# Four small edits around the FFN of a two-layer streaming encoder: stores begun from ScalarE, one more tile buffer, a split priority, two planned waits

## The chip, the cores and the metric

The kernel runs on one core of a Trainium2 chip. The metric is the device time of one execution in microseconds; a kernel's time is the median over its runs. All arithmetic is 32-bit: a product of two 32-bit operands is made of three TensorE matmuls on float32r parts (high x high, high x low, low x high), so every weight and every activation that goes into a matmul is first split into a rounded high part (a cast on ScalarE) and the remainder (a subtraction on VectorE).

## The reference

One step of a hybrid encoder on 1024 prompt rows and 64 sample rows (1088 columns here, since the kernel keeps everything transposed), width 1024, FFN width 2816. Layer 0 is a Mamba-2 SSD mixer and a SwiGLU FFN, layer 1 is chunk-band attention and a SwiGLU FFN; every sub-layer has a norm before and after.

```python
def rmsnorm(x, w):
    y = x * lax.rsqrt(jnp.mean(x * x, axis=-1, keepdims=True) + EPS)
    return y * w
def swiglu(u, w_in, w_out):
    g, up = jnp.split(u @ w_in, 2, axis=-1)
    return (jax.nn.silu(g) * up) @ w_out
for layer in range(2):
    nw = norm_w[layer]
    m = ssd_mixer(rmsnorm(x, nw[0]), ...) if layer == 0 else attention(rmsnorm(x, nw[0]), ...) @ w_o
    x = x + rmsnorm(m, nw[1])
    x = x + rmsnorm(swiglu(rmsnorm(x, nw[2]), ffn_w_in[layer], ffn_w_out[layer]), nw[3])
```

## The kernel before

**Order.** TensorE's program order is written out by hand: the Python code emits its instructions one after the other, and a planner (`Stream`, `st`) keeps a planned time `st.t` that grows with every matmul. Side tasks (generators) yield a delay in planned microseconds and go on when `st.t` has passed it; what such a task then emits for TensorE stands at that place in its order. The other queues (VectorE, ScalarE, GpSimd and the DMA issues of SyncE) are ordered by a scheduler at build time, by readiness and by emission order; `tc.high_priority(n)` lets an instruction count as emitted `n` places earlier. Every queue is then executed in order. `paced` ties an instruction to TensorE's present place, for the scheduler only.

**Columns.** The 1088 columns stand in four slices `QS` of 256, 256, 288 and 288 (q = 0 to 3), two blocks `b` of 512 and 576 (b = 0 holds q = 0 and 1), and, for the projections, three slices `SL`.

**First FFN stage** (`back`). The 22 tiles of the hidden width are worked in three groups. `T_PLAIN`, six tiles (0, 1, 2 and 11, 12, 13), is multiplied in the ordinary way for the first block only (`plain_pairs`, L1385 gate, L1389 product). `T_BOTH`, 16 tiles, goes through `run_pair` for both blocks; `T_TAIL`, which is the same six tiles as `T_PLAIN`, goes through `run_pair` for the second block. `run_pair` makes one gate tile and one up tile of both halves of a block by seven half-size products in the manner of Strassen, in the order P1, P6, P2, P7, P5, P4, P3. VectorE takes each product out of PSUM: P7 into `u3` (L1436), P5 into `c22` and `u2` (L1439, L1440), P4 (L1442 to L1444), P3 (L1446, L1447). The px pool has four PSUM tiles. The tiles `u3` of the first block share their two buffers with the second column half `x` of the plain tiles (tag `u30`).

**Hidden tiles** go to a scratch in HBM, `hscr` (`hidden`, `out`, `store`, L1475): for a tile of the first half (number below 11) two stores, the value and a difference; for a tile of the second half five stores, two values and three sums that GpSimd makes (L1481). A store is spawned with a planned delay of 4.0. The second stage reads the scratch back (L1512) and splits it (L1518, L1519).

**Weights** (`Weights`): loads into two raw tiles (L283, SyncE), sums of them for the seven products (L332, L333, L350, L351), and splits (`part`, L386 cast on ScalarE, L387 subtraction on VectorE) under `tc.high_priority(self.pri)`. `pri` is `HIP` = 3000 at the turn to paired tiles, 0 in most of the first stage and `LDP` in the second FFN stage.

**Second FFN stage.** Seven products over 11 tiles each, for both blocks (`po`, L1756 to L1758), the last of them, P4, first for block 0 and then for block 1, with weights held in the tiles `r`. As a slice's result is complete, `end` normalises it (L1584), adds the residual (L1585) under `tc.high_priority(ENP[q])`, `ENP` = (1000, 2500, 1500, 800), and stores it. In layer 0 `end` goes on to split the result for the projections (L1540, L1541), sums its squares (L1610 to L1616, `ssum`), and, after a planned wait `EQ_W[q]`, emits the second root: TensorE transposes the sums (L564, `nst`), VectorE makes the inverse root (L575 to L588, `nv`, `nr`), TensorE spreads it (L594, `nbp`) and ScalarE copies it (L597). The keys, values and queries of slice s are scaled by it (`evk`, L1898).

Of the kernel before, what the change touches and what calls it, by code (L numbers as in the profile page):

```python
# [8 lines left out]
F32 = mybir.dt.float32  # L9
# [7 lines left out]
P = 128  # L17
# [30 lines left out]
ST_W, ST_RB = (6.5, 22.0, 22.0), (6.0, 1.0, 1.0)  # L48
TB_W, TB_V = 1.0, 10.0
OS = 1.9, 1.4  # L50
EP_W, ER_W, EQ_W = (6.0, 5.0, 8.0, 6.0), (6.0, 4.0, 6.0, 5.0), (8.0, 9.0, 18.0, 16.0)

HIP = 3000
BYP = 0, 0, 800, 800
CHP, OPP = ((300, 1500), (1500, 1500)), ((0, 1200), (1200, 1200))
LDP, ENP, ATP = 1500, (1000, 2500, 1500, 800), 1000
RWP = 3000, 0, 0

KBUF, NPRE = 5, 3
# [10 lines left out]
T_PLAIN = tuple(t for k in range(NB0 // 2) for t in (k, k + KH))  # L70
T_BOTH = tuple(t for k in range(NB0 // 2, KH) for t in (k, k + KH))
T_TAIL = tuple(range(NB0 // 2)) + tuple(range(KH, KH + NB0 // 2))
HO = 0, 256
# [349 lines left out]
def hybrid_kernel(  # L423
# [4 lines left out]
    nc = tc.nc  # L428
    V, A, G, PE = nc.vector, nc.scalar, nc.gpsimd, nc.tensor
# [3 lines left out]
    def pool(es, name, bufs=1, **kw):  # L433
        return es.enter_context(tc.tile_pool(reuse_waits="tile", name=name, bufs=bufs, **kw))
# [49 lines left out]
    def paced(x):  # L484
        if at_pe[0] is not None:
            tc.add_manual_dep(x.ins, at_pe[0].ins.name, NS, reason="pace")
        return x
# [28 lines left out]
    def mm(name):  # L516
        return pmm.tile([P, 512], F32, tag="mm", name=name)
# [212 lines left out]
    with ExitStack() as es:  # L730
# [413 lines left out]
        for s in range(NSL):  # L1144
            us, n = u[s], SL[s][1]
# [251 lines left out]
    def run_pair(t_, pr, bs, ends, ops, hid, px, tmp, apart=False, keep=None):  # L1397


        tb = {b: {} for b in bs}  # L1400
        for (p_, key, c0, i), b in [(x, b) for b in bs for x in PRODS] if apart else [(x, b) for x in PRODS for b in bs]:
            h, v = pr[key]
            n, x = ops[b].n, tb[b]

            def t_new(tag):
                if tag == "u3" and keep is not None:
                    return keep[:, t_ * n:(t_ + 1) * n]
                return tmp.tile([P, n], F32, tag=f"{tag}{b}", bufs=2 if tag == "u3" or (tag == "p1" and not b) else 1, name=tag)

            st.wait_for(lambda: i in ops[b].hl)  # L1410
            ah, al = ops[b].hl[i]
            ps = (px.tile([P, 512], F32, tag="mm", name="px") if p_ != P1 else mm("px"))[:, :n]
            for k in range(4):
                wh, wl = h[:, c0 + k * P:c0 + (k + 1) * P], v[:, c0 + k * P:c0 + (k + 1) * P]
                PE.matmul(ps, wh, ah[:, k, :], start=(k == 0), stop=False)  # L1415
                PE.matmul(ps, wh, al[:, k, :], start=False, stop=False)  # L1416
                at_pe[0] = PE.matmul(ps, wl, ah[:, k, :], start=False, stop=(k == 3))  # L1417
                if k == 1:
                    st.run(6 * n / MMR)
            st.t += 6 * n / MMR  # L1420
            if b in ends:
                for r in ops[b].rings[i]:
                    r.put()
            with tc.high_priority(HIP):
                if p_ == P1:
                    x["p1"] = t_new("p1")
                    A.copy(x["p1"], ps)
                elif p_ == P6:
                    x["u2"] = t_new("u2")
                    V.tensor_tensor(x["u2"], ps, x["p1"], op=ALU.add)  # L1430
                elif p_ == P2:
                    V.tensor_tensor(x["p1"], ps, x["p1"], op=ALU.add)
                    A.activation(x["p1"], x["p1"], AF.Silu)
                elif p_ == P7:
                    x["u3"] = t_new("u3")
                    V.tensor_tensor(x["u3"], ps, x["u2"], op=ALU.add)  # L1436
                elif p_ == P5:
                    x["c22"] = t_new("c22")
                    V.tensor_tensor(x["c22"], ps, x["u3"], op=ALU.add)  # L1439
                    V.tensor_tensor(x["u2"], ps, x["u2"], op=ALU.add)  # L1440
                elif p_ == P4:
                    V.tensor_tensor(ps, ps, x["u3"], op=ALU.add)  # L1442
                    A.activation(ps, ps, AF.Silu)
                    V.tensor_tensor(x["u3"], ps, x["c22"], op=ALU.mult)  # L1444
                else:
                    V.tensor_tensor(ps, ps, x["u2"], op=ALU.add)  # L1446
                    V.tensor_tensor(x["c22"], ps, x["p1"], op=ALU.mult)  # L1447
                    hid(t_, b, x["c22"], x["u3"])
            st.pump()
            if p_ in (P2, P7, P4, P3) and b == bs[-1]:  # L1450
                W.put(p_ == P3)
# [3 lines left out]
    def back(layer, start, cpost, xsrc, xmid, cpre, cpost2, xout, rb_out, done2):  # L1455

        hc = hc_[layer]
        dn, ops, phase, hid, kept, stored = [], [Ops(0, layer), Ops(1, layer)], [0], {}, {}, {}
        with ExitStack() as es:
# [6 lines left out]
            def hidden(t_, b, x, z, late=None):  # L1466

                kh, k = divmod(t_, KH)
                n = ops[b].n

                def out(i, t):
                    st.spawn(store(i, t), HST)

                def store(i, t):
                    paced(nc.sync.dma_start(hc[:, i, k, HO[b]:HO[b] + n], t))  # L1475
                    stored[i, b] = stored.get((i, b), 0) + 1
                    return
                    yield

                def total(t, x_, y_, op):  # L1480
                    G.tensor_tensor(t, x_, y_, op=op)  # L1481
                    return t

                if not kh:
                    s3 = stage[0]()[:, :n] if late is None else late[:, k * n:(k + 1) * n]
                    out(OPI["a11"], x)
                    out(OPI["s3"], total(s3, x, z, ALU.subtract))
                    kept[k, b] = z, s3
                    return
                z0, s3 = kept.pop((k, b))  # L1490
                out(OPI["a12"], x)
                out(OPI["a22"], z)
                out(OPI["s1"], total(z0, z0, z, ALU.add))
                s2 = total(stage[0]()[:, :n], z, s3, ALU.subtract)
                out(OPI["s2"], s2)
                out(OPI["s4"], total(stage[0]()[:, :n], x, s2, ALU.subtract))
# [132 lines left out]
            with e2:  # L1629
                tmp = pool(e2, f"tm{layer}")  # L1630
# [105 lines left out]
            for x, (p_, bs) in enumerate(SEQ):  # L1736
# [4 lines left out]
                for j in range(4):  # L1741
                    keep = len(bs) == 1 and j > 0
                    ws = held.pop(j, [])
                    for b in bs:
                        n = ops[b].n
# [102 lines left out]
    with ExitStack() as es:  # L1848
# [312 lines left out]
        for j in range(1, 8):  # L2161
# [11 lines left out]
            while left:  # L2173
# [11 lines left out]
                s, i = now  # L2185
# [159 lines left out]
```

## Time and profile before

| | |
|---|---|
| median of 3 runs | 2914.41 us (2912.35 to 2919.4) |
| profiled execution | 2915.64 us, its span 2913.9 us |
| TensorE busy | 2849.0 us (98%) |
| VectorE busy | 2235.8 us (77%) |
| ScalarE busy | 1347.6 us (46%) |
| GpSimd busy | 749.7 us (26%) |
| granted TensorE clock | 0.996 |
| second queue view: hardware queue q1 | 281280 packets, 428.98 MB |

PE is TensorE, PEld its weight loads, DVE VectorE, ACT ScalarE, POOL GpSimd, SP SyncE; a q behind the name means the engine's sequencer, which issues DMAs. A row of the timeline is: start in us, length in us, engine, line of the kernel, operation, written tile <- read tiles, shapes, count, and in brackets the idle time of the engine before it and what ended it. A row of waits is: who <- whom, us in total, how often, the longest. The stages in the order of time: SSD mixer to about 690 us, then the turn to the FFN, first FFN stage of layer 0 (about 845 to 1333), second stage (to about 1573), attention (to about 2105), and the same FFN stages of layer 1 (first to about 2665, second to the end).

### The profile page before, as it was taken

How to read it: one execution, taken by the hardware profiler on the slowest of the kernel's cores; microseconds unless marked ns; L12 is line 12 of the kernel's file. 1: busy time of each engine (PE TensorE's matmuls, PEld its weight loads, DVE VectorE, ACT ScalarE, POOL GpSimd, SP SyncE). 2: the span in 40 equal slices, each digit the busy share in tenths (PEclk: the TensorE clock that was granted, in tenths of full speed). 3: DMA queues.
4: the chain of work that ended last, by engine and by line, in shares of the span. 5: the costliest groups of instructions: out<-in, count | busy, mean ns of one | idle time of the engine just before them, and what ended most of it. 6: DMA issues, size and time to landing. Idle time of an engine off the chain costs nothing.

```text
span 2913.9 us, 57802 instructions
## 1 busy us (share of the span) xinstructions
PE 2849.0 (98%) x22096; PEld 2803.5 (96%) x22096; DVE 2235.8 (77%) x4767; ACT 1347.6 (46%) x2411; POOL 749.7 (26%) x927
## 2 busy tenths in 40 slices
PE   8999999999998999999999999999999999999998
PEld 8999999999998999999998899999999999999998
DVE  7887888885768877787678777777778877787556
ACT  6654546454453222235444555565664222234442
POOL 1333333331123434341021000000032434343012
PEclk9999999999999999999999999999999999999999
DMA  4433333344565454558875432223367454566654
GB/s 139 129 97 101 107 101 103 94 126 148 178 177 149 153 179 158 184 174 268 292 230 178 132 94 72 65 67 90 105 209 209 146 176 149 181 200 204 194 176 151
DMA packets 284790, 443.22 MB, mean 152 GB/s; under 512 B 25697, under 2 KB 231489, under 8 KB 283105
## 3 DMA queue, kind: packets, MB, share of 16 engines
q1 hardware_dynamic: 281280, 428.98, 46.3%
q0 software_dynamic: 3232, 10.56, 2.0%
q8 instruction: 173, 2.83, 0.4%
q14 instruction: 105, 0.85, 0.1%
HBM read 321.34 MB, written 113.63 MB: 149 GB/s over the span
## 4 chain that ended last, share of the span: by engine, by line
PE 76%; DVE 12%; DMA 6%; ACT 3%; issue 2%; POOL 1%; SPq 0%; DVEq 0%; ACTq 0%; POOLq 0%
PE px L1416 8%; PE px L1417 8%; PE px L1415 8%; PE mm L531 7%; PE mm L533 7%; PE mm L532 7%; PE po L1758 4%; PE po L1757 4%; PE po L1756 4%; PE mmx L532 2%; PE mmx L533 2%; PE mmx L531 2%; PE ptp L2020 2%; PE po L2055 1%; DVE hl L387 1%
## 5 line engine op out<-in xcount | busy, mean ns | idle before, releaser
L531 PE MATMUL mm<-r,hl 128*128 128x384 f32 (+2 forms) x1672 | 555.2, 332 | 4.4 <-DVE kf L1898 2.5
L533 PE MATMUL mm<-r,hl 128*128 128x384 f32 (+2 forms) x1672 | 537.7, 322 | 1.8 <-DMA hl<-in_w_in_dram 1.1
L532 PE MATMUL mm<-r,hl 128*128 128x384 f32 (+2 forms) x1672 | 537.5, 321 | 0.0
L1416 PE MATMUL px<-r,hl 128*128 128x288 f32 (+1 forms) x1184 | 349.1, 295 | 0.0
L531 PEld LDWEIGHTS mm<-r,hl 128*128 128x128 f32 x1672 | 315.0, 188 | 8.1 <-DVE kf L1898 3.1
L1415 PE MATMUL px<-r,hl 128*128 128x288 f32 x1056 | 312.0, 295 | 7.7 <-DVE u L1440 4.5
L533 PEld LDWEIGHTS mm<-r,hl 128*128 128x128 f32 x1672 | 314.3, 188 | 2.4 <-DMA hl<-in_w_in_dram 1.4
L532 PEld LDWEIGHTS mm<-r,hl 128*128 128x128 f32 x1672 | 315.2, 188 | 0.3
L1417 PE MATMUL px<-r,hl 128*128 128x288 f32 x1056 | 313.1, 296 | 1.4 <-DVE hl L387 1.4
L387 DVE TENSOR_TENSOR hl<-raw,hl 128x1024 fp32r<-128x1024 f32 (+2 forms) x186 | 211.8, 1140 | 117.2 <-ACT hl L386 116.8
L557 POOL TENSOR_TENSOR ssum<-ssum,sq 128x256 f32<-128x256 f32 (+1 forms) x111 | 122.0, 1100 | 574.4 <-ACT sq L556 557.6
L386 ACT CAST hl<-raw 128x1024 fp32r<-128x1024 f32 (+2 forms) x186 | 177.5, 954 | 116.7 <-PE po L1758 65.1
L1416 PEld LDWEIGHTS px<-r,hl 128*128 128x128 f32 x1184 | 223.7, 189 | 0.0
L1417 PE MATMUL px<-rx,hl 128*128 128x256 f32 x768 | 215.7, 281 | 5.6 <-DVE hl L387 5.5
L1415 PE MATMUL px<-rx,hl 128*128 128x256 f32 x768 | 215.2, 280 | 1.2 <-DVE x L1389 1.1
L1415 PEld LDWEIGHTS px<-r,hl 128*128 128x128 f32 x1056 | 200.1, 190 | 8.6 <-DVE u L1440 4.9
L1417 PEld LDWEIGHTS px<-r,hl 128*128 128x128 f32 x1056 | 200.1, 190 | 1.9 <-DVE hl L387 1.9
L1756 PE MATMUL po<-r,hl 128*128 128x288 f32 (+1 forms) x682 | 196.6, 288 | 0.0
L1757 PE MATMUL po<-r,hl 128*128 128x288 f32 (+1 forms) x682 | 196.4, 288 | 0.0
L1758 PE MATMUL po<-r,hl 128*128 128x288 f32 (+1 forms) x682 | 196.4, 288 | 0.0
L1416 PE MATMUL px<-rx,hl 128*128 128x256 f32 x640 | 179.2, 280 | 0.0
L2004 ACT ACTIVATE sc<-sc,mx 128x640 f32<-128x640 f32 (+3 forms) x144 | 101.8, 708 | 107.7 <-DVE mx L1999 102.7
(444 smaller groups left out, 8424.4 us busy)
## 6 DMA issues: line engine op xcount, KB each, us to landing
raw<-in_w_f_dram SPq DMA_DIRECT2D x104, 512.0 KB, 4.0
wsum<-in_w_f_dram SPq DMA_DIRECT2D x128, 176.0 KB, 3.7
wscr<-wsum SPq DMA_DIRECT2D x128, 176.0 KB, 3.3
raw<-in_w_in_dram SPq DMA_DIRECT2D x40, 512.0 KB, 3.7
MT<-ascr SPq DMA_DIRECT2D x48, 384.0 KB, 4.3
raw<-in_w_so_dram SPq DMA_DIRECT2D x32, 512.0 KB, 3.9
r<-hscr SPq DMA_DIRECT2D x22, 576.0 KB, 5.8
hl<-kscr SPq DMA_DIRECT2D x11, 1024.0 KB, 5.6
```

The costliest lines, as they stand in the source:

```text
L386: self.nc.scalar.copy(h, v)
L387: (eng or self.eng or self.nc.vector).tensor_tensor(lo, v, h, op=ALU.subtract)
L531: PE.matmul(ps[:, :n], h_, xh, start=(first and i == 0), stop=False)
L532: PE.matmul(ps[:, :n], h_, xl, start=False, stop=False)
L533: at_pe[0] = PE.matmul(ps[:, :n], l_, xh, start=False, stop=(last and i == nk - 1))
L557: (eng or G).tensor_tensor(ssum[:, :n], ssum[:, :n], q[:, :n], op=ALU.add)
L1415: PE.matmul(ps, wh, ah[:, k, :], start=(k == 0), stop=False)
L1416: PE.matmul(ps, wh, al[:, k, :], start=False, stop=False)
L1417: at_pe[0] = PE.matmul(ps, wl, ah[:, k, :], start=False, stop=(k == 3))
L1756: PE.matmul(ps[:, :n], wh, xh, start=(k == 0), stop=False)
L1757: PE.matmul(ps[:, :n], wh, xl, start=False, stop=False)
L1758: at_pe[0] = PE.matmul(ps[:, :n], wl, xh, start=False, stop=(k == KH - 1))
```

## The change

1. The DMA that stores a hidden tile is issued by ScalarE (`A`) instead of SyncE if the tile's number is in `T_PLAIN`. The number is all that is asked, so it holds for the plain tiles of block 0 and for the tail tiles of block 1.
2. The tile `c22` of the second block gets two buffers instead of one.
3. `LDP` goes from 1500 to 2000.
4. `EQ_W` goes from 8.0 to 16.0 for slice 0 and from 9.0 to 11.5 for slice 1 (it is used in layer 0 alone).

```diff
-EP_W, ER_W, EQ_W = (6.0, 5.0, 8.0, 6.0), (6.0, 4.0, 6.0, 5.0), (8.0, 9.0, 18.0, 16.0)
+EP_W, ER_W, EQ_W = (6.0, 5.0, 8.0, 6.0), (6.0, 4.0, 6.0, 5.0), (16.0, 11.5, 18.0, 16.0)
...
-LDP, ENP, ATP = 1500, (1000, 2500, 1500, 800), 1000
+LDP, ENP, ATP = 2000, (1000, 2500, 1500, 800), 1000
...
-                return tmp.tile([P, n], F32, tag=f"{tag}{b}", bufs=2 if tag == "u3" or (tag == "p1" and not b) else 1, name=tag)
+                return tmp.tile([P, n], F32, tag=f"{tag}{b}", bufs=2 if tag == "u3" or (tag == "p1" and not b) or (tag == "c22" and b) else 1, name=tag)
...
-                    paced(nc.sync.dma_start(hc[:, i, k, HO[b]:HO[b] + n], t))
+                    paced((A if t_ in T_PLAIN else nc.sync).dma_start(hc[:, i, k, HO[b]:HO[b] + n], t))
```

## The prediction

> **What bounds the kernel now.** First the page, for the share of each engine; then the waits of TensorE (PE), since PE is busy nearly throughout and only its waits can be won; then, for each wait that an edit touches, the tile view of the FFN scratch and the timeline of the engine it waits for.
>
> ```profile
> span 2913.9 us, 57802 instructions
> ## 1 busy us (share of the span) xinstructions
> PE 2849.0 (98%) x22096; PEld 2803.5 (96%) x22096; DVE 2235.8 (77%) x4767; ACT 1347.6 (46%) x2411; POOL 749.7 (26%) x927
> ```
>
> PE stands for 2913.9 - 2849.0 = 65 us. No edit takes a matmul away, so nothing beyond those 65 us is to be had. The waits of PE (us in total, times, longest) say which part the edits can reach:
>
> ```profile
> PE po L1758 <- DVE hl L387: 5.0, 3, 3.1
> PE px L1415 <- DVE u L1440: 4.5, 2, 2.4
> PE px L1415 <- DVE u L1436: 3.2, 2, 2.2
> ...
> PE mmx L531 <- ACT x L1385: 1.9, 2, 1.7
> ...
> PE po L1756 <- ACT r L386: 1.2, 1, 1.2
> ...
> PE nst L564 <- DVE ssum L1616: 0.8, 1, 0.8
> PE po L1758 <- DVE r L387: 0.8, 1, 0.8
> ```
>
> Each of these I follow to its cause; the larger waits at the turn from plain to paired tiles, for splits of FFN weights, no edit aims at. The view of the scratch tile shows who waits for its transfers (last three rows: us, times), and how long SyncE (SP) is taken by one issue (ns min/median/max):
>
> ```profile
> L1475 SPq DMA_DIRECT2D hscr<-x x24: 319/436/1002, 866.5 to 2266.1; - x24
> ...
>   DVE c L1439: 10.0, 8
>   DVE u L1436: 9.6, 3
>   ACT x L1385: 6.4, 1
> ...
> DMA to landing us min/median/max: 1.7/4.0/11.0
> ```
>
> So VectorE (DVE) and ScalarE (ACT) stand until a tile's store has landed and the tile may be written again. A store can land in 1.7 us; the median is 4.0.
>
> **Stores begun from ACT.** The condition is on the tile number, so it takes the 21 stores of the six plain tiles (three with 2, three with 5) and the 21 of the same tiles in the tail of the second block: 42 a layer, 84 in all. They leave SP, where each took 0.44 us in the middle, and stand in ACT's queue instead. Three places where a late store of these tiles holds an engine:
>
> ```profile
> 876.12 0.42 DVE L1389 TENSOR_TENSOR x<-mmx,x 128x256 f32<-128x256 f32 x1
> 878.74 1.87 POOL L1481 TENSOR_TENSOR sg<-x,sg 128x256 f32<-128x256 f32 x2
> 885.32 1.96 SPq L1475 DMA_DIRECT2D hscr<-x  x3
> 891.33 0.94 ACT L1385 ACTIVATE x<-mmx 128x256 f32<-128x256 f32 x3 [6.36 <-DMA hscr<-x]
> 939.04 0.42 DVE L1436 TENSOR_TENSOR u<-px,u 128x256 f32<-128x256 f32 x1 [6.48 <-DMA hscr<-x]
> 2269.41 0.43 DVE L1436 TENSOR_TENSOR u<-px,u 128x256 f32<-128x256 f32 x1 [2.39 <-DMA hscr<-x]
> ```
>
> GpSimd (POOL) finished the last sum of a tile at 878.74 + 1.87 = 880.6, but SP, in order, issued this tile's stores only from 885.32, behind a residual store and two weight loads. ACT's next gate stood 6.36 us for them and PE lost the 1.7 of its waits. Stores in ACT's queue do not stand behind those loads: issued at about 881 and landed after 1.7 to 5 us they are gone before the gate wants its tile at 891.33 - 6.36 = 885, or little later. The waits at 939.04 and 2269.41 are the same thing at the first paired tile: its fourth product needs a tile whose store SP holds back. PE lost 3.2 in the two. Gain 1.7 + 3.2 = 4.9; bounds 0 (the stores land no sooner) and 4.9.
>
> What it costs: ACT now waits for POOL's sums where SP did, and gates, copies and weight casts queue behind. A tile of the second half has five stores. From DVE's result (876.12 + 0.42 = 876.5) to POOL's last sum are 4.1 us, and a last issue of 0.44 makes 4.5 if ACT stands from the start. The cover is the row at 891.33: ACT stood 6.36 and PE lost 1.7, so 4.7 passed without loss. Held 4.5, nothing is lost; held with four more issues behind the wait, 6.3, it is 1.6. There are 12 tiles with five stores, so the bounds are 0 and 19; the list order puts a store where its data is expected, nearer the lower end, and I take a third of a us for each, 4.0, which also stands for the new order of the queues around. POOL's own work is unchanged; SP's loads behind the stores start sooner, which I cost at nothing, since PE waits at the loads named above for other reasons.
>
> The Trainium skill speaks against this edit: "Perfetto Trace Analysis", section "DMA Instruction — HWDGE (DVE, Sync)", says that the issuing sequencer is free for its next instruction only after the generator was locked and all descriptors were made, and that the profile's duration leaves out the wait for the data. By that rule 84 issues take 84 x 0.44 = 37 us of ACT's queue whatever they wait for. The durations above agree that an issue has a length; whether ACT's and SP's locks collide no run here shows. That ACT has room for them is in the next row, so the sum is the same with the rule or without.
>
> ```profile
> core 0: us, PE busy (x) PEld busy (x) DVE busy (x) ACT busy (x) POOL busy (x), PEclk, DMA share, GB/s
> ...
> 1268.00:1333.00 65.00, 61.47 (x463) 61.00 (x462) 54.04 (x80) 29.52 (x43) 29.89 (x24) 1.00 0.65 201
> ```
>
> The row is the tail of the first layer: ACT is busy 29.5 of 65 us; DVE, with 54 of 65, has far less room.
>
> **Second buffer for the gate tile c22 of the second block.** With one buffer, DVE's write for the next pair waits until the last pair's store has landed:
>
> ```profile
> 1271.45 0.72 SPq L1475 DMA_DIRECT2D hscr<-c  x1
> 1278.18 0.46 DVE L1439 TENSOR_TENSOR c<-px,rx 128x288 f32<-128x288 f32 x1 [1.75 <-DMA hscr<-c]
> 2609.80 0.46 DVE L1439 TENSOR_TENSOR c<-px,rx 128x288 f32<-128x288 f32 x1 [0.62 <-DMA hscr<-c]
> ```
>
> The store of the last two-block pair is issued at 1271.45 behind reloads of the scratch, DVE stands 1.75 us, and holds the PSUM tile that PE wants next; PE loses 4.5 in the two layers (longest 2.4). That pair's stores stay on SP, so only the buffer helps here. It gives DVE back 1.75 and 0.62; what PE gains beyond that depends on whether DVE, which is full just behind with weight splits, does this write earlier than other work. I take DVE's idle time, 2.4; bounds 0 and 4.5, and not below, since it only lifts a wait. Next late is the split of weights that follows.
>
> **Splits ahead of ENP (LDP 1500 to 2000).** In the second FFN stage a weight split has now the same head start, 1500 places, as the post-norm of the third slice (ENP[2]).
>
> ```profile
> 2862.23 0.72 ACT L386 CAST hl<-raw 128x640 fp32r<-128x640 f32 x1
> 2863.27 1.34 DVE L1585 TENSOR_TENSOR y<-y,xq 128x1152 f32<-128x1152 f32 x1
> 2867.09 0.81 DVE L387 TENSOR_TENSOR hl<-raw,hl 128x640 fp32r<-128x640 f32 x1
> 2867.96 0.58 PE L1758 MATMUL po<-rx,hl 128*128 128x256 f32 x1 [3.06 <-DVE hl L387]
> 1536.93 0.38 PE L1758 MATMUL po<-rx,hl 128*128 128x256 f32 x1 [1.56 <-DVE hl L387]
> ```
>
> ACT has cast the weights at 2862.95, but DVE runs the third slice's normalisation (L1585 and the products around it) and makes the low part only at 2867.09; PE stands 3.06 us. In layer 0 the same happens, 1.56 us, and then the loads that wait for DVE to release their buffers come late: the 1.2 and 0.8 of waits at r. With 2000 the split goes at 2863 to 2864, before PE arrives at 2867.96 - 3.06 = 2864.9. The slice's chain is put back by 0.81 a split, two or three splits; its output is not the last one, and its second root has 18 us of its own. Gain 3.06 + 1.56 + 1.2 + 0.8 = 6.6, which I take, since cast and post-norm lie open side by side. Bounds 6.6 and, if the split was not yet ready in the scheduler's order, 0; -2.4, three splits, if PE came to wait for the slice's chain. The third wait of that row, 0.4, stays.
>
> **Second roots later.** In layer 0 the sums of slice 0 are read by PE 8 planned us later and those of slice 1 by 2.5. The first wait, 0.8 at ssum, goes. The other is the first of these rows:
>
> ```profile
> 1583.54 0.41 PE L564 MATMUL nst<-ident,ssum 128*128 128x128 f32 x2 [1.08 <-DVE nv L586]
> 1584.75 0.29 PE L594 MATMUL nbp<-ident,nr 128*128 128x128 f32 x1 [0.80 <-DVE nr L588]
> ```
>
> Two transposes later PE stands again, for a root of the last slice. With the first moved past the second, PE arrives there earlier and waits for the same root (DVE). I take 0; bounds -2.5, if the first keys then wait for their root, and 1.1. The root of slice 0 is wanted only with that of slice 1, when the first keys are scaled, so its own delay costs nothing; the cover is the products of the first two slices that PE makes before.
>
> **Sum.** 4.9 - 4.0 + 2.4 + 6.6 + 0.8 = 10.7. The profiled execution took 2915.6 (span 2913.9 and 1.7 around it): 2904.9. The median of the three runs, 2914.4, is 1.2 below that execution, so 2903.7, or 2904.
>
> **The rivals.** (1) DVE gives it back: freed waits are only turned into waits for the next DVE result, since DVE is the fuller engine at each place. Then c22 brings nothing and the splits half: 4.9 - 4.0 + 3.3 + 0.8 = 5.0, 2909. For it: 54 of 65 us busy in the tail. Against: in the second FFN stage order is changed, not amount. (2) The priority does not do what it says: the split came late because the planner held it for later, not by rank. Without the 6.6: 4.1, 2910. For it: the split at 2867.09 lies inside a stretch where the chain could not go on. (3) The stores land no sooner, since the transfers around them fill the engines: without the 4.9, 5.8 stay, 2909. For it: the landing median of 4.0 against 1.7 alone. The Trainium skill has this rule ("DMA: Bandwidth & Descriptors", section "Issuing engines are not separate DMA queues"): begun from several engines, transfers still share the same engines and only issue time is saved; the 4.7 us between the sum at 880.6 and the issue at 885.3 are such time. (4) On the other side: ACT, in order, stands for POOL's sums in front of a copy or gate that PE needs at once. Place: the five stores of a second-half tile. It decides from 14.7 / 12 = 1.2 us of PE a tile; if the five issues alone are uncovered, 5 x 0.44 = 2.2 a tile, 26 us, it ends at 2914 + 12 = 2926. Against: the 4.7 us of cover.
>
> **How the numbers follow.** The forecast has 0.52, (1) 0.20, (2) 0.12, (3) 0.07, (4) 0.09. About 0.3%, 8.7 us, is what a measurement of this kernel can tell from no change: faster means below 2905.7, slower above 2923.1. The forecast lies below, (1) to (3) within, (4) above: 0.52, 0.39, 0.09. The forecast's own range is 2897 (all terms full, c22 at 4.5, ACT at no cost: 2914.4 - 16.8) to 2906. For 8 in 10 I leave out part of both ends and take in (1) to (3) with some of ACT's cost: 2898 to 2913.
>
> **What would show it.** Right: the list of DMA queues has a second hardware queue; no gate L1385 and no L1436 waits for hscr; the rows at u L1440 and u L1436 are gone from PE's waits, po <- hl L387 falls from 5.0 to under 1, and the nst wait at ssum L1616 is gone. PE's busy time stays near 2849 and its idle time falls to about 54. Wrong: PE waiting for ACT x L1385, p L1427 or hl L386 with ACT held by POOL; new waits at kf L1898 if a root is late; or idle time of PE that is the same in sum and only has other names.

## The result and the profile after

The changed kernel takes 2906.18 us (median; 2901.95 to 2908.31) beside 2915.6 for the kernel before on the same chip: ratio 0.9965, 95% interval 0.9953 to 0.9977, or 9 to 10 us less. The forecast was 2904.0 with 10.7 less. Two profiled executions of experiments below were disturbed as a whole (5656 and 9920 us); they are left out, and those two kernels were traced once more.

The first part of the page, and the list of DMA queues (packets, MB, share of 16 engines; one row of it):

```profile
span 2900.2 us, 57727 instructions
PE 2843.5 (98%) x22096; PEld 2799.6 (97%) x22096; DVE 2242.8 (77%) x4767; ACT 1347.7 (46%) x2411; POOL 763.6 (26%) x927
...
q10 hardware_dynamic: 12096, 11.70, 1.2%
```

TensorE (PE) idles 56.7 us instead of 64.9, and it is busy 5.5 us less with the same 22096 matmuls, which the forecast did not foresee. Queue q10 is new: ScalarE's (ACT's) 84 stores. The waits of TensorE (us in total, times, longest):

```profile
PE px L1417 <- DVE hl L387: 11.9, 7, 2.4
PE mm L531 <- DVE kf L1898: 5.0, 2, 4.3
PE nbp L594 <- DVE nr L588: 4.8, 5, 1.6
...
PE px L1415 <- DVE u L1430: 1.6, 2, 1.4
...
PE po L1758 <- DVE r L387: 1.2, 2, 1.0
...
PE po L1758 <- DVE hl L387: 0.9, 1, 0.9
```

Of the waits that the change aimed at one remains, the one at r L387, with 1.2 us instead of 0.8. The others are gone: no row at u L1440, u L1436, gate L1385 or ssum L1616, and po <- hl L387 is down from 5.0 to 0.9. In the view of the scratch tile no gate and no L1436 waits any more. But other rows have grown since before, two of which were:

```profile
PE px L1417 <- DVE hl L387: 6.9, 5, 2.4
...
PE mm L531 <- DVE kf L1898: 2.5, 2, 1.8
```

Five more us stand at the weight splits, 2.5 at kf and 2.6 at nbp (2.2 before). Subtracting the start of the same matmul in the two traces shows where: TensorE is 6.4 us ahead after the plain tiles of layer 0 (1.2 of them from stages before), 12.0 when that layer's second stage ends, only 6.8 when attention is under way, and 13.7 at the end. So the turn to layer 1 gives 5 back. (At the first keys the lead reads 14.7, but there the matmuls of the roots have moved from before them to behind them, so the two orders differ.) In the tails the lead first grows and then falls: 6.9, 9.1, 6.2 in layer 0 and 11.6, 13.3, 9.9 in layer 1. Two places to ask about, then: the tails, where new waits stand at the splits and at u L1430, and this turn.

### The profile page after: what moved, and what is told of

It is laid out like the page before. It is cut to its first block, busy times and chain, and to the rows that moved or that the text cites. A ratio compares the mean times of both kernels' runs of the same rounds, so it can differ in the third digit from the quotient of the medians.

```text
span 2900.2 us, 57727 instructions
## 1 busy us (share of the span) xinstructions
PE 2843.5 (98%) x22096; PEld 2799.6 (97%) x22096; DVE 2242.8 (77%) x4767; ACT 1347.7 (46%) x2411; POOL 763.6 (26%) x927
## 5 line engine op out<-in xcount | busy, mean ns | idle before, releaser
L1417 PE MATMUL px<-r,hl 128*128 128x288 f32 x1056 | 312.4, 296 | 5.4 <-DVE hl L387 5.4
L387 DVE TENSOR_TENSOR hl<-raw,hl 128x1024 fp32r<-128x1024 f32 (+2 forms) x186 | 209.5, 1128 | 118.4 <-ACT hl L386 118.1
L1417 PE MATMUL px<-rx,hl 128*128 128x256 f32 x768 | 214.8, 280 | 6.5 <-DVE hl L387 6.5
L1417 PEld LDWEIGHTS px<-r,hl 128*128 128x128 f32 x1056 | 199.4, 189 | 6.4 <-DVE hl L387 6.4
```

Source lines behind the costliest of these rows:

```text
L387: (eng or self.eng or self.nc.vector).tensor_tensor(lo, v, h, op=ALU.subtract)
```

## Experiments

"Undone" kernels take one edit out of the changed kernel, the others go on from it or from the kernel before. All ratios are to the kernel before on the same chip, with 95% intervals; a difference of two ratios carries both intervals, added in squares.

| kernel | edit | median us | ratio |
|---|---|---|---|
| changed | all four | 2906.2 | 0.9965 [0.9953, 0.9977] |
| u_store | stores undone | 2909.0 | 0.9971 [0.9961, 0.9981] |
| u_c22 | buffer undone | 2913.0 | 0.9990 [0.9979, 1.0001] |
| u_ldp | priority undone | 2912.8 | 0.9989 [0.9980, 0.9998] |
| u_eq | second roots undone | 2907.3 | 0.9969 [0.9958, 0.9981] |
| a_c22 | buffer alone | 2911.8 | 0.9987 [0.9977, 0.9997] |
| plain | no tail stores on ScalarE | 2900.8 | 0.9941 [0.9926, 0.9957] |
| tail_nosum | tail: only VectorE's tiles | 2899.5 | 0.9947 [0.9933, 0.9960] |
| kqv3 | third key/query/value buffer | 2901.8 | 0.9949 [0.9933, 0.9965] |
| best | plain and kqv3 | 2895.5 | 0.9924 [0.9910, 0.9938] |
| fill | best, four waits filled | 2889.2 | 0.9910 [0.9896, 0.9923] |

**Stores undone.**

```diff
-paced((A if t_ in T_PLAIN else nc.sync).dma_start(...))
+paced(nc.sync.dma_start(...))
```

> The changed kernel with all stores on SyncE's queue again; the other three edits stay. Forecast's theory (4.9 gained, 4.0 paid on ScalarE): about 0.9 of the 9.4 us is lost, ratio to before about 0.997; the waits at the gate L1385 (1.7) and at L1436 (3.2) come back, and the new waits of TensorE in the two tails (px <- hl L387, px <- u L1430) go. Theory from the two traces (in the tails ScalarE stands for GpSimd's sums and gives back what the second gate buffer won): 5 to 8 us come back in the plain tiles, and each tail ends 3 to 4 us earlier, net 0 to 2 lost. Rival: the tails give back because VectorE is full there, whoever issues the stores: 5 to 8 us lost, ratio 0.999, and the gaps at the ends of the tails stay.

1.7 us are lost by the times, with 4.6 on either side. Its waits:

```profile
PE px L1415 <- DVE u L1436: 5.5, 2, 2.9
...
PE mmx L531 <- DVE x L1389: 1.8, 1, 1.8
...
PE mmx L531 <- ACT x L1385: 0.7, 1, 0.7
```

The waits at L1436 are back with 5.5. In layer 0 a late store holds the gate tile again (ScalarE stands 5.9 us for it), and TensorE stands 1.8 at the product behind it; in layer 1 it stands 0.7 at a gate. The late gaps of the tails, at u L1430 and at the last split, are gone with ScalarE's stores, as both the forecast and the second theory had it; the rival that the tails give back whoever issues the stores falls. Net the edit is worth little, because it wins in one place and pays in the other.

**Tail stores back on SyncE, those of the first block's plain tiles on ScalarE.**

```diff
-(A if t_ in T_PLAIN else nc.sync)
+(A if t_ in T_PLAIN and not b else nc.sync)
```

> The changed kernel with ScalarE issuing only the stores of the plain tiles of the first block; the tail's 42 stores are SyncE's again. Forecast's theory (ScalarE pays a third of a us in each tile with five stores, six of the twelve lie in the tails, and all of the 4.9 gained lies in the plain tiles): 2 us better than the changed kernel, ratio 0.9958, TensorE's waits near the end of each tail (px <- u L1430, the last px <- hl L387) gone. Rival (SyncE's reloads of the scratch then stand behind those stores, as in the undo run, where the split at the tail's start came 0.7 us later): no change, 0.9965, or 2 worse.

> The version with ScalarE's stores only in the first block's plain tiles, once more for its trace. Theory that its 7 us over the changed kernel are ScalarE standing for GpSimd's sums in the tails: in both tails the waits px <- hl L387 and px <- u L1430 are shorter by 2 to 4 us a layer, and no cast L386 or copy L1427 stands for a sum L1481; in the plain tiles the trace is as that of the changed kernel. Rival: the 7 us come from a stage without such stores (the clock, or the turn to the next layer), and the tails take as long as before.

7.0 us less than the changed kernel, give or take 5.7; the traced execution took 2904.81. Without tail stores on ScalarE the waits of the two tails are one each:

```profile
PE px L1417 <- DVE hl L387: 2.0, 1, 2.0
...
PE px L1417 <- DVE hl L387: 2.7, 1, 2.7
```

These are answers for the stretches 1200 to 1345 and 2540 to 2665 us. In the changed kernel the same stretches held:

```profile
PE px L1417 <- DVE hl L387: 2.3, 2, 1.5
PE px L1415 <- DVE u L1430: 1.4, 1, 1.4
...
PE px L1417 <- DVE hl L387: 3.2, 2, 2.4
```

With 0.2 more at u L1430 in the second tail that is 7.1 against 4.7: 2.4 us of waits, close to the 2 expected at first and short of the 2 to 4 a layer expected of the trace. Matmul by matmul, the wait at the head of each tail stands in both kernels and is no shorter without the stores (2.0 and 2.7, beside 1.5 and 2.4). What goes is u L1430 and the last split of each tail (0.7 each); both stand in all five traces in which ScalarE stores GpSimd's sums in the tails, and in no other. The mechanism at the last split of the first tail, in the changed kernel's timeline (start, length, engine, and in brackets what ended the idle time before):

```profile
1308.15 1.25 POOL L1481 TENSOR_TENSOR rx<-rx,u 128x288 f32<-128x288 f32 x1
...
1309.43 0.33 ACTq L1475 DMA_DIRECT2D hscr<-rx  x1
...
1311.35 1.51 POOL L1481 TENSOR_TENSOR sg<-c,sg 128x288 f32<-128x288 f32 x1
...
1312.89 0.33 ACTq L1475 DMA_DIRECT2D hscr<-sg  x1
...
1313.26 1.05 ACT L386 CAST hl<-raw 128x1024 fp32r<-128x1024 f32 x1 [0.22 <-issue]
...
1314.34 1.23 DVE L387 TENSOR_TENSOR hl<-raw,hl 128x1024 fp32r<-128x1024 f32 x1 [0.51 <-ACT hl L386]
...
1315.62 0.40 PE L1417 MATMUL px<-r,hl 128*128 128x288 f32 x1 [0.72 <-DVE hl L387]
```

The store of a sum goes only when GpSimd (POOL) has it: that at 1309.43 behind 1308.15 + 1.25, that at 1312.89 behind 1311.35 + 1.51. Behind it in ACT's queue stands the cast of the next weights; VectorE's low part follows, and TensorE stands 0.72. In the trace without these stores the same cast comes right behind the copy L1427:

```profile
1311.60 0.39 ACT L1427 COPY p<-px 128x288 f32<-128x288 f32 x1
1311.89 1.06 ACT L386 CAST hl<-raw 128x1024 fp32r<-128x1024 f32 x1
```

What holds u L1430 was not followed. The time says 7.0 with a lower end of 1.3. By the starts of the same matmuls, from the head of each tail until well into the second stage, both tails together win 0.2 us in this trace, 3.4 in that of the next experiment, and 3.1 from kqv3 to best. The place is shown, then, and the size is open.

**In the tail, ScalarE issues only the stores of tiles that VectorE wrote.**

```diff
+(A if t_ in T_PLAIN and (not b or i in (OPI["a11"], OPI["a12"], OPI["a22"])) else nc.sync)
```

> The changed kernel in which, in the tails, ScalarE still issues the 18 stores of tiles that VectorE wrote, and SyncE the 24 of GpSimd's sums. Theory that ScalarE loses by standing for the sums: as good as without any tail store on ScalarE, ratio 0.9941 (0.993 to 0.995). Rival that it loses by the time of the issues themselves, in proportion: 18 of 42 of the 7 us stay, ratio 0.9951. Rival that stores on SyncE delay its reloads: between that and 0.9965.

The ratio lies 0.0006 above that of plain, with 0.0021 on either side: the times do not tell the first two theories apart. The trace speaks for the first: one wait in each tail (1.9 and 2.2), as without any store on ScalarE, though nine issues a layer stay in its queue.

**Second buffer undone, and alone.**

```diff
-(tag == "p1" and not b) or (tag == "c22" and b) else 1
+(tag == "p1" and not b) else 1
```

> The changed kernel with one buffer for the gate tile c22 of the second block again. Forecast's theory: the wait at L1439 (1.75 and 0.62 of VectorE) comes back and 2.4 us are lost, ratio 0.9974. Rival (nothing kept): in the changed kernel's trace the 2.7 and 3.9 us won at the place of this buffer are given back before the tail ends, so the time does not change (0.9965), and both the gain at the first pairs of the tail and the later loss are missing from the trace.

> The kernel before with the second buffer for c22 of the second block as its only change. Forecast's theory: 2.4 us gained, ratio 0.9992. Rival from the undo run (7.3 us lost there, with an interval of some 4 on either side): VectorE's wait also delays the weight splits behind it and TensorE loses more than VectorE stands, so 5 to 7 us are gained, ratio 0.9977 to 0.9983. Second rival: the buffer pays only where ScalarE issues the tail's stores, and alone it gives nothing, 1.000.

Undone, 7.3 us are lost (4.7 on either side); alone, 3.8 are won (2.9 on either side). By the starts of the same matmuls, undoing costs 2.5 us from the head of the first tail into the second stage and 2.7 in layer 1, and nothing of it comes back before the tail ends: "nothing kept" falls, and so, by the times, does "alone it gives nothing". (2.0 of the first come back later, by the turn to layer 1.) Alone, the same reading gives 3.0 and 0.1. The waits of the kernel with the buffer alone show what takes the place of u L1440, as the prediction had put it ("next late is the split of weights that follows"):

```profile
PE px L1417 <- DVE hl L387: 10.7, 6, 2.4
```

**Priority undone.**

```diff
-LDP = 2000
+LDP = 1500
```

> The changed kernel with the split priority at 1500 again. Forecast's theory: 6.6 us are lost, ratio 0.9988; TensorE's wait po <- hl L387 is back at 3 or more waits of 1.5 to 3 us in the second FFN stage, in both layers. Rival (given back): in layer 0 TensorE is up to 14.7 us early when the next layer's attention begins and gives 8 of it back there; if that stretch is bound by something that does not move with TensorE, the 4 us of layer 0 are lost anyway, and undoing costs only layer 1's share, 2 to 3 us, ratio 0.9974.

7.0 us are lost (4.4 on either side). The row po <- hl L387 is back:

```profile
PE po L1758 <- DVE hl L387: 4.7, 2, 3.2
```

Of TensorE's lead, 3.0 us are lost in the second FFN stage of layer 0 and 5.1 in that of layer 1, and layer 0's share is not made up at the turn. Both the rival of the prediction (the priority does not do it) and that of the expectation (given back) fall.

**Second roots undone.**

```diff
-EQ_W = (16.0, 11.5, 18.0, 16.0)
+EQ_W = (8.0, 9.0, 18.0, 16.0)
```

> The changed kernel with the second roots of slices 0 and 1 at their old due times (8.0 and 9.0). Forecast's theory: 0.8 us lost, one wait at ssum L1616. Theory from the two traces: the later roots make the first keys of layer 1 late (TensorE waits 4.3 us at kf L1898 and 2.7 at nbp, which were 1.8 and 1.1), so undoing them gains 3 to 6 us, ratio 0.9945 to 0.9955. Rival: that stretch is held by transfers (the store of the value tile, the rope table's load) whatever the roots do; then TensorE arrives as early, waits as long, and the time does not change.

> The changed kernel with the old due times of the second roots, for its trace. Forecast's theory: the wait at ssum L1616 (0.8) is back and nothing else moves, so TensorE's wait at kf L1898 stays at about 4.2. Theory that the later roots make the first keys late: kf L1898 falls to about 2 and the two waits at nbp (1.56 and 1.16) go.

By the times 1.2 us are lost, with 4.8 on either side: nothing that can be told. The trace (2897.89 us in that execution) shows why:

```profile
PE mm L531 <- DVE kf L1898: 2.6, 2, 1.8
PE nst L564 <- DVE ssum L1616: 2.5, 1, 2.5
```

With the old due times the wait at ssum is 2.5, not 0.8, since TensorE now comes there some 10 us earlier than in the kernel before; kf falls from 5.0 to 2.6 and the long waits at nbp go. Each setting pays in another place. Neither theory is right as it stood: the later roots do lead to the wait at kf, but undoing them wins nothing. Set side by side, the traces with two key buffers also say what the turn gives back: the six with the new due times have 4.3 to 5.0 us at kf, the three with the old ones 2.5 or 2.6. The kernel with the stores undone is among the six (4.9), though its TensorE comes to the turn as late as that of the kernel before (10.6 and 11.1 us behind the changed kernel). So the wait came with the due times and not with the lead.

**Third buffer for keys, queries and values.**

```diff
-tile([P, 384], F32, tag="kqv", bufs=2, ...)   # kf, qf and vt
+tile([P, 384], F32, tag="kqv", bufs=3, ...)
```

> The changed kernel with three buffers instead of two for the key, query and value tiles at the start of the next attention. Theory: VectorE stands 3.46 us there for the store of a value tile, TensorE then 4.30, and its clock is lower for 19 matmuls behind it (2.05 more); with a third buffer VectorE goes on and 3 to 6 us are gained, ratio 0.9944 to 0.9955. Rival: ScalarE, which stands 7.64 us for the context load cr at the same place, holds the key tiles' casts and so the buffers all the same: at most 1 us gained, ratio 0.9962 to 0.9965, and the wait at kf L1898 stays near 4.

The changed kernel's timeline at the turn:

```profile
1595.53 0.36 SPq L492 DMA_DIRECT2D out_vT_dram<-vt  x1
...
1600.29 0.56 DVE L1924 SCALAR_TENSOR_TENSOR qf<-kq,rbf 128x384 f32<-128x384 f32 x1 [3.46 <-DMA out_vT_dram<-vt]
...
1600.63 0.62 ACT L1869 CAST Ck<-cr 64x512 fp32r<-64x512 f32 x1 [7.64 <-DMA cr<-in_ckT_dram]
...
1601.16 1.04 ACT L1905 CAST K<-kf 64x384 fp32r<-64x384 f32 x2
...
1601.80 1.14 DVE L1906 TENSOR_TENSOR K<-kf,K 64x384 fp32r<-64x384 f32 x2
...
1603.45 0.54 DVE L1898 TENSOR_TENSOR kf<-mm,rbf 128x384 f32<-128x384 f32 x1
...
1604.05 0.64 PE L531 MATMUL mm<-r,hl 128*128 128x320 f32 x1 [4.30 <-DVE kf L1898]
```

The value tile's store is issued at 1595.53, behind two loads of bias rows; VectorE wants one of the two buffers for the next query and stands 3.46 us until that store has landed. The key that TensorE waits for (1603.45) comes behind it, and TensorE stands 4.30. ScalarE stands 7.64 for the context at the same time, with the cast of the keys behind it (1601.16); the low parts at 1601.80 need that cast and stand ahead of the key in VectorE's queue. With three buffers, the waits and two rows of ScalarE:

```profile
PE mm L531 <- DVE kf L1898: 0.7, 1, 0.7
...
1601.20 1.05 ACT L1905 CAST K<-kf 64x384 fp32r<-64x384 f32 x2 [3.00 <-DVE kf L1898]
...
1607.16 1.26 ACT L1869 CAST Ck<-cr 64x512 fp32r<-64x512 f32 x2
```

The wait at kf is 0.7 in all. But two things changed at once: the query no longer waits for the store, and the build has put the cast of the keys ahead of that of the context, for which ScalarE now stands not at all. Which of the two held the key is not shown. The second has its signs: the keys stand ahead of the context in ScalarE's queue in the three traces with the old due times as well, and in all six with the new ones the context comes first, with a stand of 7.2 to 7.9 us. By the starts of the same matmuls TensorE is 7.0 us behind the changed kernel ahead of the turn (slow stretches early in that execution) and 0.7 behind after it: 6.3 won, 4.3 of them the waits at kf and most of the rest the clock behind them. That TensorE is late here is not what wins it: the kernel best, which is 1.5 ahead of the changed kernel before the turn, is 7.7 ahead after it. The row at nbp stays as it was. The times give 4.7 with 5.8 on either side.

**Both together.**

```diff
+ the edits of plain and of kqv3
```

> ScalarE's stores only in the first block's plain tiles, and three buffers for the key, query and value tiles; the other three edits of the change stay. If the two gains lie at different places and add: 7.0 and 4.6 us below the changed kernel, ratio 0.9925, some 2895 us. Rival: the next layer's start is bound by what comes next (the context load on ScalarE), and an earlier arrival there is given back: 0.994.

As expected if the two add: 0.9924, some 12 us below the changed kernel (5.4 on either side).

**Filling four waits.**

```diff
+if p_ == P5 and (apart and not b or bs == (1,) and t_ == T_TAIL[1]):
+    for _ in range(8):
+        PE.matmul(pf[:, 384:512], ones, ones, start=True, stop=True)
```

> The version with ScalarE's stores in the first block's plain tiles and three key, query and value buffers, and in addition eight matmuls of a constant into unused columns of the product's own tile ahead of the fifth product of the first paired tile and of the second tail tile, in both layers: work that nobody reads, in the four waits at px <- hl L387 (2.36, 2.08, 2.36, 2.30 us, behind which TensorE's matmuls were slow for 1.6, 1.6, 2.6 and 1.6 us more). Theory that the clock drops because TensorE idled over 2 us: the four waits shrink to under 1, no slow stretch follows them, and about 7 us less are taken than without the filling, ratio 0.990. Rival: the slow stretches have another cause and stay, or the filling only puts the real matmuls back: ratio 0.9924 or up to 3 us worse.

Four stretches of best and of fill, each around one of the waits (columns: busy us and count for PE, PEld, DVE, ACT, POOL, then granted clock, DMA share, GB/s):

```profile
918.00:935.00 17.00, 13.55 (x98) 13.18 (x97) 11.23 (x17) 5.35 (x9) 7.47 (x7) 0.90 0.54 154
1265.00:1285.00 20.00, 17.93 (x124) 17.69 (x123) 18.40 (x27) 8.85 (x13) 11.32 (x8) 0.91 0.70 235
2235.00:2256.00 21.00, 16.77 (x117) 16.20 (x117) 20.91 (x23) 10.34 (x13) 8.91 (x6) 0.84 0.37 110
2592.00:2608.00 16.00, 13.70 (x93) 13.46 (x92) 15.70 (x22) 6.41 (x10) 8.63 (x6) 0.89 0.68 231
```

```profile
918.00:935.00 17.00, 14.91 (x124) 14.31 (x123) 14.05 (x20) 6.59 (x10) 8.62 (x7) 1.00 0.45 127
1265.00:1285.00 20.00, 19.47 (x150) 19.24 (x150) 17.91 (x25) 9.94 (x15) 7.53 (x6) 1.00 0.80 267
2235.00:2256.00 21.00, 18.30 (x148) 17.32 (x147) 20.91 (x23) 10.27 (x13) 8.93 (x6) 1.00 0.38 110
2592.00:2608.00 16.00, 15.82 (x121) 15.38 (x120) 14.04 (x20) 5.16 (x9) 8.71 (x6) 1.00 0.61 203
```

```profile
PE px L1421 <- DVE hl L387: 3.9, 6, 1.4
```

(The inserted lines move L1417 to L1421.) The clock is 1.00 in all four instead of 0.84 to 0.91, no slow stretch follows, and the waits at the splits fall from 10.8 to 3.9 us. By the starts of the same matmuls the four places win 1.6, 1.1, 1.5 and 1.6 us, 5.8 in all, so the filling does not only put the real matmuls back. The ratio is 0.9910, 4.1 us below best with 5.7 on either side: by the times the size is open, in the trace the mechanism is shown four times out of four. It is the best version run.

## Why the prediction was right

**Stores, +4.9 and -4.0.** The two halves are real and lie where they were put, but the price is in the tails alone. All waits of TensorE in the plain stages (855 to 945 and 2195 to 2280 us) sum to 13.4 us in the kernel before and 9.0 in the changed one, 4.4 less; they sum to 16.0 with the stores undone and to 10.1 in the trace with those of the plain tiles, 5.9 less. The 4.9 lies between, though 1.6 to 1.8 of what went stood at the product x L1389, which the forecast had not counted. ScalarE's price shows as 2.4 us of waits in the tails, 0.4 for each of their six tiles with five stores, where a third of a us was taken, because there casts of weights that TensorE needs next stand behind the stores. In the plain tiles the cover of 4.7 us held: the waits at the splits there are 6.5 us in the changed kernel, as with the stores undone (5.5 before), so nothing that can be told was paid. Rival (4) named this mechanism; its 1.2 us a tile were not reached. Rival (3), stores that land no sooner, falls with the waits at the gate and at L1436. The rule of the Trainium skill in "Perfetto Trace Analysis", section "DMA Instruction — HWDGE (DVE, Sync)", is not decided here: 18 issues in the tail cost nothing that can be told, and ScalarE had room.

**Buffer, +2.4.** Mis-sized: 3.1 us alone and 5.2 in the company of the other edits by the traces, 3.8 and 7.3 by the times. VectorE's idle time was too small a measure; in company TensorE's loss (4.5, the upper bound) was nearer.

**Priority, +6.6.** As forecast: 7.0 by the times. Of the 8.1 of lead that the trace without it loses, some 2.7 are slow stretches behind its longest wait, which leaves 5.4; the rows of waits in the two second stages differ by 5.2. The 0.8 at r L387 that the sum counted here did not go. Rival (2) falls.

**Second roots, +0.8.** Nothing to tell from zero, as a sum; the step's own words ("two transposes later PE stands again") were right, but the price came by another way than its bound of -2.5, a late root. The keys wait 2.5 us longer at kf and the roots 2.6 longer at nbp; the key stands behind a store and behind ScalarE's casts, whose order changes with the due times, and the step looked at neither.

**What the sum left out** are the clock behind a wait and the waits that came back at the turn; the two have opposite signs. Between the two profiled spans lie 13.7 us: 8.2 of waits, where the sum had 10.7, and 5.5 of busy time, where it had none ("PE's busy time stays near 2849" was wrong). The traced execution of the changed kernel lies 4.2 below its median, so of the 5.5 hardly more than 1 is in the medians' difference, if the waits are the same in the others. The sign named for late roots, "new waits at kf L1898", did appear, though what held the key was no root. Rival (1), that freed waits only turn into waits for the next DVE result, holds in part: the row of weight splits grew by 5.0. That 10.7 comes so near to the 9.4 measured is thus in part luck: the stores and the buffer won more than their terms, and the turn took some 5 us back. The four losses of the undone kernels add to 17.2 us where the whole change is worth 10; each of them carries the changed kernel's own 3.5 on either side, which is why the sizes here are taken from the traces where they show them.

## What to carry to other kernels

Move a store to an engine whose next work nobody waits for: here the same edit won in one stage and lost in another, and was worth most when split by stage. When a due time is moved, compare the order of every queue at the next turn with the order before: here the wait that grew at the turn came with the due times, and it looked like a lead given back. Before a row is called the mechanism, see whether the same matmul waits in the kernel without the edit. Price a TensorE wait of 2 us or more as the wait and what the clock takes behind it, and fill it with idle matmuls where nothing better is to be had.

## What the hardware showed beyond what was expected

A wait of TensorE goes on behind its end: the matmuls that follow are slow for a while. In the changed kernel the wait of 2.36 us that ends at 926.05 is followed, some matmuls later, by such that are half as long again (0.28 and 0.42) and start 0.22 us apart instead of 0.12:

```profile
926.05 0.38 PE L1417 MATMUL px<-rx,hl 128*128 128x256 f32 x1 [2.36 <-DVE hl L387]
...
926.51 0.28 PE L1417 MATMUL px<-rx,hl 128*128 128x256 f32 x1
926.63 0.28 PE L1415 MATMUL px<-rx,hl 128*128 128x256 f32 x1
...
927.57 0.42 PE L1417 MATMUL px<-rx,hl 128*128 128x256 f32 x1
927.79 0.42 PE L1415 MATMUL px<-rx,hl 128*128 128x256 f32 x1
```

In twelve traces, leaving out the first 100 us, the norms at 646 us and attention, 41 of 50 waits of 2 us or more had such a stretch within 1.6 us, costing some 1.2 to 3 us; of the waits between 1.75 and 2 us 8 of 13 had one; of 54 waits of 1.0 to 1.74 us only six, each with a wait of about 2.4 just behind it. So there is no sharp bound in these traces: the longest wait without such a stretch is one of 2.73. (A stretch is counted where matmuls start over 1.3 times as far apart as the same pair does in the middle.) The Trainium skill, "TensorE: Matmul & The Clock Gate", section "What's actually happening", has the clock fall to one half after an idle window of about 3.4 us. The trace agrees on the kind of thing and not on the length: waits of about 2 us were mostly enough. It goes with the scatter of the times: of thirty runs of the kernel before, five at a granted clock of 0.993 took 2920.9 us on average, and seven at 0.996 took 2914.0.
